# Making the next block's input from the scaled old residual and the scaled y, high parts first

## The chip, the cores and the metric

The kernel runs on one core of one Trainium2 chip. The metric is device time in microseconds (us): the median of several executions. Engines are named as the profile names them: PE (TensorE matmul), PEld (its weight loads), DVE (VectorE), ACT (ScalarE), POOL (GpSimd) and SP (the queue that issues the DMAs).

## What is computed

Two transformer blocks follow each other. The first works on two streams of 256 tokens, `x` and a context; the second on `x` alone. Cut to what matters here, the end of the first block and the start of the second are:

```python
ux = _modulate(_rmsnorm(hx, g[2]), mx[:, 3], mx[:, 4])
yc, yx = _neighbourhood_attention(uc, ux, ...)             # last mixer of the first block
hx = hx + mx[:, 5] * _rmsnorm(yx, g[3])                    # join A
hx = _ffn_sublayer(hx, (mx[:, 6], mx[:, 7], mx[:, 8]), g[4], g[5], ...)   # x alone
# second block, for l in range(2):                           join B stands before l = 0
h = rmsnorm(x, norm_w); proj = h @ w_in
...                                                        # MLA, gated delta rule, MoBA
x = x + y @ w_out                                          # join C: l = 0 into l = 1
```

Everything is fp32. A matmul operand is kept as a high part and a low part, and a product is made of three matmuls: high by high, weight high by input low, weight low by input high.

## The kernel before

The residual `h` lies in SBUF as 8 slices (k = 0 to 7) of 128 features by 256 tokens for `x`. A sublayer leaves its output `y` in two tiles of four slices, and the sums of its squares as matmuls by a matrix of ones into PSUM bank `n`. What joins two sublayers runs in this order where only `x` is left:

- `rstd` (L358): ACT L371 makes a first 1/sqrt from bank `n`, DVE refines it in three steps (L372 to L374). This is r of y.
- `add_normed` (L385): per two slices, DVE multiplies y by the gain column and r (L393, twice 256 wide) and adds it to `h` (L397, 512 wide).
- `scaled` (L444): per slice ACT writes the high part of h times the next norm's gain column (L459) and DVE the low part (L460). The next input's own r is not multiplied in: it is applied behind the matmuls. For it ACT squares two slices of `h` (L64), and `Sums(self, True)` feeds each square to PE at once, two fp32 matmuls by ones per square, eight in all.
- `ffn` (L474) or `hybrid` (L1171) then projects. In `ffn` for `x` alone, f = 0 to 11 first: two weight tiles, two PSUM banks of the tag `ab` (three banks; `ac` has four), 48 matmuls 258 wide, then `part` (L487): DVE multiplies both banks by r (L510, L513), ACT applies Silu, and the result is split again. In `hybrid`, `prn(i)` loads weight i, projects into a `pj` bank (two) or a `gd` bank (three) in 24 matmuls, and DVE multiplies by a copy `rk` of r (L1176, L1182); four-tap convolutions on DVE (L1043), Silu on ACT, the gates and the delta rule follow. The gates' first matmuls are those of L197 into `gd`.

Weights come by DMA as 128x1024 tiles and are split by ACT (high part, L173) and DVE (low part, L174) into a pool of eight tiles, four weights. A scheduler orders the instructions of each engine when the program is built; on the chip every engine takes them strictly in that order.

The three places where this joining happens with `x` alone are called A (neighbourhood attention into the last `ffn`, at about 1620 us), B (that `ffn` into hybrid layer 0, at about 1830 us) and C (hybrid layer 0 into layer 1, at about 2028 us; there is no y norm, only `scaled`).

Of the kernel before, what the change touches and what calls it, by code (L numbers as in the profile page):

```python
# [83 lines left out]
class Net:  # L84
# [359 lines left out]
    def scaled(self, cols, shift=None):  # L444


        nc = self.nc
        u = self.new_u(1 if shift is None else 2)
        if shift is not None:
            for b, s in enumerate(u[1]):  # L450
                self.split(shift[:, 2 * b:2 * b + 2].unsqueeze(2).broadcast_to([128, 2, 2]), s.hi[:, :, 256:258],
                           s.lo[:, :, 256:258])
        ss = Sums(self, True)
        for b in range(4):
            for t in range(2):
                k = 2 * b + t
                hi, lo = self.us(u, k, 0, 256)
                h = self.h[:, k, 0:256]
                nc.scalar.activation(hi, h, AF.Copy, scale=cols[:, k:k + 1])  # L459
                nc.vector.scalar_tensor_tensor(lo, h, cols[:, k:k + 1], hi.bitcast(F), op0=OP.mult, op1=OP.subtract)  # L460
            ss.add(self.hs(0, b, 2))
        return u, ss.rstd()

    def columns(self, r):

# [8 lines left out]
    def ffn(self, n, u, halves, mid, xdone, extra=(), r=None):  # L474
# [9 lines left out]
            s = g[f // 2]  # L484
            return s.hi[:, f % 2, c0:c1], s.lo[:, f % 2, c0:c1]

        def part(f, ws, c0, c1):  # L487
            w = c1 - c0
            if w == 512 or r is not None:
                (pa, pb), ab = [self.bank("ab") for _ in range(2)], None  # L490
            else:
                p = self.bank("ab", (128, 2, 256))
                pa, pb, ab = p[:, 0], p[:, 1], {}
            w2 = w if r is None else w + 2
            for k, p, wt in [(k, *x) for x in zip((pa, pb), ws) for k in range(DT)] if r is None else \
                    [(k, *x) for k in range(DT) for x in zip((pa, pb), ws)]:
                self.mm3([p[:, :w2]], wt.at(lambda x: x[:, k * 128:(k + 1) * 128]), [self.us(u, k, c0, c0 + w2)],
                         k == 0, k == DT - 1, [ab])
            if f // 2 not in g:
                t = self.bp.tile([128, 2080], R, name="b", tag="b")  # L500
# [29 lines left out]
        with self.space("ffn", 6):  # L530
# [10 lines left out]
            def wide(f):  # L541
# [3 lines left out]
                    next(extra)  # L545
                part(f, ws, 0, width)

            for f in range(f0, FA):
                wide(f)

# [40 lines left out]
    def proj(self, src, u, c0, c1, tag="ab", m=128):  # L591
        w = self.weight(src, 8 * m)
        p = self.bank(tag)[:m, :c1 - c0]
        self.project(p, w, u, c0, c1, m)
        return p

    def project(self, p, w, u, c0, c1, m=128, bank=None):
        for k in range(DT):
# [572 lines left out]
    def hybrid(self, l, scaled, prm3):  # L1171
# [4 lines left out]
        nc.vector.tensor_copy(rk, r)  # L1176
        cw, prm, abt = prm3
        W = I["w2"]
        def prn(i, out=None, scale=1.0, tag="pj"):
            p = self.proj(W[l, i], u, 0, 256, tag)  # L1180
            out = self.r1() if out is None else out
            nc.vector.scalar_tensor_tensor(out, p, scale, rk, op0=OP.mult, op1=OP.mult)  # L1182
            return out
# [131 lines left out]
    def program(self):  # L1315
# [14 lines left out]
        with self.psum(pj=2, gd=3, at=2), self.narrow_space(), self.space("hy", 1):  # L1330
            self.second_consts()
            cols = [self.n2[:, l] for l in range(3)]
            if on("s"):
                for l in range(2):
                    self.hybrid(l, self.scaled(cols[l]), prm[l])
                    self.save(f"d_s{l}")
            ss = Sums(self, True)
            for b in range(4):
# [12 lines left out]
    def first_block(self, es, on, ada):  # L1351
# [11 lines left out]
        with self.psum(ab=3, ac=4):  # L1363
# [51 lines left out]
            for i, (name, l, which, factor, halves, run) in enumerate(seq):  # L1415
# [7 lines left out]

                def xdone(y, l=l, which=which, factor=factor, nxt=nxt, box=box):
                    if nxt and nxt[4] == 1 and nxt[0] != "na":
                        link(None, y, 0, (l, which, factor), None)
                        box["u"] = self.scaled(*self.pre_cols(*nxt[1:3], 0))
                    elif nxt:
                        box["u"] = self.new_u()
                        link(box["u"], y, 0, (l, which, factor), nxt[1:3])  # L1430
                    else:
                        link(None, y, 0, (l, which, factor), None)

                yc = run(u, mid, xdone)
                post = (l, which, factor)
# [143 lines left out]
```

## Time and profile before

| | |
|---|---|
| median of 3 runs (lowest, highest) | 2234.25 us (2233.92, 2235.57) |
| the profiled execution: its own time | 2232.82 us |
| the profiled execution: span of the trace | 2230.8 us |
| busy share of the span: PE, PEld | 97%, 84% |
| busy share: DVE, ACT, POOL | 71%, 50%, 0% |
| chain that ended last, by engine | PE 79%, ACT 9%, DVE 9%, issue 1%, DMA 1% |

The trace lists every instruction of one execution with its start, its length and what released its engine if it stood idle before. A window row gives the busy time of each engine in a stretch, and the clock granted to PE as a share of full speed.

### The profile page before, as it was taken

Reading aid. Unit: us, or ns where it says so; the run is one execution under the profiler, and the core shown is the slowest. Engines: PE = TensorE matmul, PEld = TensorE weight load, DVE = VectorE, ACT = ScalarE, POOL = GpSimd, SP = SyncE. Lnnn points to the kernel's source line nnn. Section 1 sums busy time; section 2 is a strip of 40 time slices with the busy share of each in tenths; the row PEclk is TensorE's granted clock in tenths of the full one; section 3 lists DMA queues with packets and bytes.
Section 4 is the critical chain, followed back from the end, with each engine's and each line's share of the span. In section 5 each row is a group of like instructions: output and inputs, shape, how many; then the busy total and the mean of one; then the engine's idle time right before and its main releaser. Section 6 shows DMA issues by size and latency. Waiting matters only on the chain.

```text
span 2230.8 us, 33424 instructions
## 1 busy us (share of the span) xinstructions
PE 2169.8 (97%) x13010; PEld 1878.0 (84%) x13010; DVE 1587.0 (71%) x2899; ACT 1117.2 (50%) x1841; POOL 6.5 (0%) x34
## 2 busy tenths in 40 slices
PE   7999999999999999999999999999999989999997
PEld 4888889877789888889988889977789989888986
DVE  7877674869978876758844454956565668977985
ACT  4422223668867322236622223668754448457744
POOL 0000000000000000000000000000000000000000
PEclk9999999999999999999999999999999999999999
DMA  8556553431135766644554453442346553324331
GB/s 303 194 183 194 181 187 124 155 104 48 38 104 166 227 202 191 196 162 149 189 172 159 161 171 132 152 132 86 109 131 188 170 171 123 114 77 142 120 99 57
DMA packets 96165, 332.76 MB, mean 149 GB/s; under 512 B 12772, under 2 KB 15462, under 8 KB 96008
## 3 DMA queue, kind: packets, MB, share of 16 engines
q1 hardware_dynamic: 96008, 330.64, 45.8%
q8 instruction: 102, 1.67, 0.3%
q14 instruction: 55, 0.45, 0.1%
HBM read 329.55 MB, written 1.05 MB: 148 GB/s over the span
## 4 chain that ended last, share of the span: by engine, by line
PE 79%; ACT 9%; DVE 9%; issue 1%; DMA 1%; SPq 0%; DVEq 0%; ACTq 0%
PE ab L182 36%; PE ac L182 16%; PE ac L186 8%; PE ab L197 5%; PE pj L182 4%; PE gd L182 3%; PE n L182 2%; PE ab L186 2%; ACT w L173 2%; DVE w L174 2%; PE at L182 1%; ACT c L795 1%; DVE y L393 1%; PE gd L186 1%; PE pj L186 1%
## 5 line engine op out<-in xcount | busy, mean ns | idle before, releaser
L173 ACT ACTIVATE w<-raw 128x1024 fp32r<-128x1024 f32 x466 | 489.5, 1053 | 785.1 <-PE ab L182 269.1
L182 PE MATMUL ab<-u,w 128*128 128x512 f32 (+2 forms) x4320 | 870.9, 361 | 4.1 <-ACT u L459 4.1
L182 PEld LDWEIGHTS ab<-u,w 128*128 128x128 f32 x4320 | 729.0, 189 | 126.1 <-ACT u L459 4.5
L174 DVE TENSOR_TENSOR w<-raw,w 128x1024 fp32r<-128x1024 f32 x466 | 565.6, 1216 | 316.2 <-ACT w L173 309.2
L182 PE MATMUL ac<-b,w 128*128 128x512 f32 (+1 forms) x1152 | 233.6, 364 | 0.0
L182 PEld LDWEIGHTS ac<-b,w 128*128 128x128 f32 x1152 | 196.4, 188 | 36.6
L186 PE MATMUL ac<-b,w 128*128 128x256 f32 x1680 | 202.1, 281 | 0.0
L186 PEld LDWEIGHTS ac<-b,w 128*128 128x128 f32 x1680 | 199.9, 189 | 0.8
L182 PE MATMUL pj<-u,w 128*128 128x256 f32 (+1 forms) x1200 | 156.1, 285 | 5.9 <-ACT u L459 4.4
L311 DVE SCALAR_TENSOR_TENSOR ra<-ra,cb 128x1024 f32<-128x1024 f32 x130 | 158.3, 1222 | 4.7 <-ACT cb L1373 2.2
L197 PE MATMUL ab<-u,w 128*128 128x256 f32 x1152 | 147.8, 290 | 7.3 <-ACT u L173 5.8
L182 PEld LDWEIGHTS pj<-u,w 128*128 128x128 f32 (+1 forms) x1200 | 145.5, 187 | 10.8 <-ACT u L459 5.0
L197 PEld LDWEIGHTS ab<-u,w 128*128 128x128 f32 x1152 | 144.0, 197 | 9.2 <-ACT u L173 6.0
L311 DVE SCALAR_TENSOR_TENSOR c<-ra,cb 128x1024 f32<-128x1024 f32 x98 | 118.8, 1219 | 14.2 <-ACT cb L1373 7.0
L507 DVE TENSOR_TENSOR s<-s,ab 128x512 f32<-128x512 f32 (+1 forms) x78 | 47.0, 603 | 90.9 <-PE ab L182 90.4
L182 PE MATMUL ac<-w,u 128*128 128x512 f32 x384 | 90.4, 393 | 0.0
L182 PEld LDWEIGHTS ac<-w,u 128*128 128x128 f32 x384 | 71.7, 188 | 15.4 <-DVE u L174 0.4
L182 PE MATMUL n<-r,ones 128*128 128x256 f32 (+1 forms) x216 | 73.7, 452 | 7.1 <-ACT r L64 2.7
L173 ACT ACTIVATE b<-s 128x512 fp32r<-128x512 f32 (+1 forms) x100 | 53.3, 533 | 29.6 <-DVE s L507 22.5
L174 DVE TENSOR_TENSOR b<-s,b 128x512 fp32r<-128x512 f32 (+1 forms) x100 | 56.2, 562 | 3.1 <-ACT b L173 2.9
L182 PEld LDWEIGHTS n<-r,ones 128*128 128x128 f32 x216 | 36.7, 197 | 19.9 <-DVE r L62 8.2
L64 ACT ACTIVATE r<-h 128x512 f32<-128x512 f32 x56 | 34.9, 626 | 31.4 <-DVE h L397 10.4
(291 smaller groups left out, 2297.0 us busy)
## 6 DMA issues: line engine op xcount, KB each, us to landing
raw<-in_fin SPq DMA_DIRECT2D x194, 512.0 KB, 3.4
raw<-in_fout SPq DMA_DIRECT2D x112, 512.0 KB, 3.4
ra<-in_ada SPq DMA_DIRECT2D x72, 512.0 KB, 4.2
ra<-in_ada0r SPq DMA_DIRECT2D x58, 512.0 KB, 3.5
raw<-in_w SPq DMA_DIRECT2D x54, 512.0 KB, 3.4
raw<-in_da_qk SPq DMA_DIRECT2D x16, 512.0 KB, 3.3
raw<-in_na_qk SPq DMA_DIRECT2D x16, 512.0 KB, 3.4
raw<-in_w2o SPq DMA_DIRECT2D x16, 512.0 KB, 3.4
```

The costliest lines, as they stand in the source:

```text
L64: net.nc.scalar.activation(s, x, AF.Square)
L173: self.nc.scalar.activation(hi, x, AF.Copy)
L174: self.anchor = self.nc.vector.tensor_tensor(lo, x, hi.bitcast(F), op=OP.subtract).ins.name
L182: return mm(out, lhsT, rhs, start=start, stop=stop)
L186: ins = mm(out, lhsT, rhs, start=start and "first" not in bank, stop=stop and bank["done"] == n)
L197: ins = mm(out, lhsT, rhs, start=start, stop=stop)
L311: ins = nc.vector.scalar_tensor_tensor(junk, w, 1.0, self.cb[:, j], op0=OP.mult, op1=OP.mult, accum_out=self.mod[l][:, m, t, j:j + 1])
L393: ins = nc.vector.scalar_tensor_tensor(yy[:, t], yy[:, t], cols[:, k:k + 1], r, op0=OP.mult, op1=OP.mult)
L507: nc.vector.tensor_tensor(s, s, pb, op=OP.mult)
L795: nc.scalar.activation(e[:, j, :nk], s, AF.Exp, bias=mx[:, j:j + 1], accum_out=sm[:, j:j + 1])
```

## The change

At A and B, `join` replaces `add_normed` followed by `scaled`. ACT scales the old residual by the next gain column (`old`, L487) and y by the product of both gain columns (`new`, L489). Once r of y is there, DVE multiplies `new` by it (L493) and adds it to `old` (L494), 512 wide; ACT copies the sum into the high part (L495), and DVE makes all low parts (L498) behind the last high part. Only then do `add_normed` and the norm of the new residual run, and the squares are added up on DVE (L62) ahead of two matmuls by ones in place of eight. `low_last` projects with the high parts of several weights at once and with the low parts after them: f = 0 and f = 1 of the `ffn` together in four banks (two `ab`, two `ac`), and the first three projections of each hybrid layer (two `pj`, one `gd`). C keeps `scaled`, with the squares added on DVE and `low_last`.

```diff
-        ss = Sums(self, True)
+        ss = Sums(self)
+    def join(self, y, ss, post, cols, shift=None):
...
+        both = self.small(DT, "both")
+        nc.vector.tensor_tensor(both, post, cols, op=OP.mult)
...
+        for k in range(DT):
+            nc.scalar.activation(at(old, k), self.h[:, k, 0:256], AF.Copy, scale=cols[:, k:k + 1])
+        for k in range(DT):
+            nc.scalar.activation(at(new, k), at(y, k), AF.Copy, scale=both[:, k:k + 1])
+        r = ss.rstd()
+        for b in range(4):
+            v = two(old, b)
+            nc.vector.tensor_tensor(two(new, b), two(new, b), r.unsqueeze(1).broadcast_to([128, 2, 256]), op=OP.mult)
+            nc.vector.tensor_tensor(v, v, two(new, b), op=OP.add)
+            nc.scalar.activation(self.part_of(u, b)[0], v, AF.Copy)
+        for b in range(4):
+            hi, lo = self.part_of(u, b)
+            nc.vector.tensor_tensor(lo, two(old, b), hi.bitcast(F), op=OP.subtract)
+        self.add_normed(y, r, post, 0)
+        return u, self.norm_r(0)
...
+            if r is not None:
+                ws = [fin(f) for f in range(2)]
+                ps = [[self.bank(tag) for _ in range(2)] for tag in ("ab", "ac")]
+                self.low_last([p[:, :258] for x in ps for p in x], sum(ws, []), u, 0, 258)
+                for f in range(2):
+                    part(f, ws[f], 0, 256, ps[f])
+                f0 = 2
...
+    def low_last(self, ps, ws, u, c0, c1):
+        at = lambda x, k: x[:, k * 128:(k + 1) * 128]
+        for k in range(DT):
+            for p, w in zip(ps, ws):
+                hi = self.us(u, k, c0, c1)[0]
+                self.mm(p, at(w.hi, k), hi, k == 0, False)
+                self.mm(p, at(w.lo, k), hi, False, False)
+        for p, w in zip(ps, ws):
+            for k in range(DT):
+                self.mm(p, at(w.hi, k), self.us(u, k, c0, c1)[1], False, k == DT - 1)
...
+        ws = [self.weight(W[l, i]) for i in range(3)]
+        ps = [self.bank(tag)[:, :256] for tag in ("pj", "pj", "gd")]
+        self.low_last(ps, ws, u, 0, 256)
...
-            p = self.proj(W[l, i], u, 0, 256, tag)
+            p = ps[i] if i < 3 else self.proj(W[l, i], u, 0, 256, tag)
...
-                    self.hybrid(l, self.scaled(cols[l]), prm[l])
+                    self.hybrid(l, self.scaled(cols[l]) if l else self.join(*self.last, cols[0]), prm[l])
...
-                        link(None, y, 0, (l, which, factor), None)
-                        box["u"] = self.scaled(*self.pre_cols(*nxt[1:3], 0))
+                        box["u"] = self.join(*y, self.post_cols(l, which, factor, 0), *self.pre_cols(*nxt[1:3], 0))
```

The scheduler's order moves with it. First ACT at join A, before the change, from the squares of the second half of y to the first high part (`ac` are the banks of that half, `r512` squares, `n` the bank of sums, `r256_14093` r of y, `w` split weights, `u` parts of the next input):

```order
L64 ACTIVATE r512_14080<-ac_13955 128x512
L687 ACTIVATE y_14077<-ac_13955 128x512
L173 ACTIVATE w_14254<-raw_14252 128x1024
L64 ACTIVATE r512_14085<-ac_13956 128x512
L687 ACTIVATE y_14077<-ac_13956 128x512
L371 ACTIVATE r256_14093<-n_13946,eps_78 128x256
L459 ACTIVATE u_14112<-h_81,pa120_14110 128x256 x2
```

The same stretch of ACT with the change:

```order
L64 ACTIVATE r512_14080<-ac_13955 128x512
L749 ACTIVATE y_14077<-ac_13955 128x512
L489 ACTIVATE y_14114<-y_13941,both_14110 128x256 x2
L64 ACTIVATE r512_14085<-ac_13956 128x512
L749 ACTIVATE y_14077<-ac_13956 128x512
L489 ACTIVATE y_14114<-y_13941,both_14110 128x256 x2
L489 ACTIVATE y_14115<-y_14077,both_14110 128x256 x4
L371 ACTIVATE r256_14133<-n_13946,eps_78 128x256
L173 ACTIVATE w_14212<-raw_14210 128x1024
L495 ACTIVATE u_14094<-c4_14112 128x2x256
```

Six scalings of y now stand between the last square and the rstd, and a weight's high part behind the rstd instead of ahead of it; its low part (`w_14213`) stands on DVE between r and the first L493.

Next DVE at join A with the change, from the sum of the third square to the first bank that is read (`ab_14216` holds half of f = 0, `r256_14181` is r of the new residual; `add_normed` and one more low part, `w_14340`, stand ahead of these rows):

```order
L62 TENSOR_TENSOR r512_14166<-r512_14166,r512_14171 128x512
L174 TENSOR_TENSOR w_14346<-raw_14343,w_14345 128x1024
L62 TENSOR_TENSOR r512_14166<-r512_14166 128x256
L62 TENSOR_TENSOR r512_14174<-r512_14174 128x256
L174 TENSOR_TENSOR w_14413<-raw_14410,w_14412 128x1024
L174 TENSOR_TENSOR w_14419<-raw_14416,w_14418 128x1024
L372 SCALAR_TENSOR_TENSOR r512_14174<-n_14178,r256_14181 128x256
L373 SCALAR_TENSOR_TENSOR r512_14174<-r512_14174,r256_14181 128x256
L374 SCALAR_TENSOR_TENSOR r256_14181<-r512_14174,r256_14181 128x256
L174 TENSOR_TENSOR w_14485<-raw_14482,w_14484 128x1024
L552 TENSOR_TENSOR s_14317<-ab_14216,r256_14181 128x256
L553 COPY s_14317<-ab_14216 128x1
```

and PE beside it, where each row of `ab` or `ac` is a number of matmuls and a row of `n` one matmul by ones:

```order
L182 MATMUL ab<-u,w 128x258 x16
L182 MATMUL ac<-u,w 128x258 x16
L182 MATMUL ab<-u,w 128x258 x10
L182 MATMUL n<-r_14166,ones 128x256
L182 MATMUL n<-r_14174,ones 128x256
L182 MATMUL ab<-u,w 128x258 x470
```

Before, the L460s were DVE's last work ahead of the r of the new residual. Now `add_normed`, the sums on DVE and five weights' low parts stand there or just behind, and on PE the sums stand inside f = 2: its first bank takes 24 matmuls into the third `ab` bank (10 ahead of the sums), its second bank is the one that L552 and L553 free.

Last, PE at join B with the change, from the end of `low_last` on (`gd`, `pj` and `at` are projections, L197 `n` turns r into columns):

```order
L182 MATMUL gd<-u,w 128x256 x34
L182 MATMUL at<-u,w 8x256 x2
L182 MATMUL gd<-u,w 128x256 x3
L182 MATMUL n<-r_16594,ones 128x256
L182 MATMUL n<-r_16602,ones 128x256
L182 MATMUL gd<-u,w 128x256 x17
L197 MATMUL n<-ones,r_16609 128x1 x2
L182 MATMUL gd<-u,w 128x256 x2
L182 MATMUL at<-u,w 8x256 x5
L182 MATMUL pj<-u,w 128x256 x48
```

In the kernel before 32 projection matmuls stood ahead of that L197, now 120 do; and the gates' first L197 into `gd` stands 456 projection matmuls into hybrid layer 0 where it stood 491 in.

## Rows read from the trace of the kernel before

**Rows 1.** The page's first part: busy time, share of the span, instructions.

```profile
PE 2169.8 (97%) x13010; PEld 1878.0 (84%) x13010; DVE 1587.0 (71%) x2899; ACT 1117.2 (50%) x1841; POOL 6.5 (0%) x34
```

**Rows 2.** Busy windows: stretch, length, PE, PEld, DVE, ACT, POOL, clock, DMA, GB/s.

```profile
1660.00:1680.00 20.00, 20.00 (x163) 19.60 (x163) 13.32 (x26) 8.87 (x13) 0.00 (x0) 1.00 0.58 180
1850.00:1910.00 60.00, 59.03 (x470) 55.25 (x468) 54.28 (x111) 54.73 (x81) 1.20 (x12) 1.00 0.48 157
1910.00:1950.00 40.00, 37.13 (x280) 34.04 (x279) 37.37 (x102) 15.36 (x26) 0.00 (x0) 1.00 0.32 95
2040.00:2100.00 60.00, 59.92 (x471) 55.80 (x470) 55.36 (x122) 51.67 (x80) 1.00 (x10) 1.00 0.44 141
```

**Rows 3.** Timeline of join A: start, length, engine, line, instruction [idle before, releaser].

```profile
1611.00 10.43 PE L186 MATMUL ac<-o,w 128*128 128x256 f32 x86
...
1622.31 0.58 ACT L64 ACTIVATE r<-ac 128x512 f32<-128x512 f32 x1
...
1622.79 0.59 ACT L687 ACTIVATE y<-ac 128x512 f32<-128x512 f32 x1
...
1624.11 0.47 ACT L371 ACTIVATE r<-n,eps 128x256 f32<-128x256 f32 x1 [0.73 <-PE n L182]
...
1625.99 0.88 DVE L393 SCALAR_TENSOR_TENSOR y<-y,po,r 128x256 f32<-128x256 f32 x2
1626.91 0.69 DVE L397 TENSOR_TENSOR h<-h,y 128x512 f32<-128x512 f32 x1
1627.52 0.87 DVE L393 SCALAR_TENSOR_TENSOR y<-y,po,r 128x256 f32<-128x256 f32 x2
1627.64 0.91 ACT L459 ACTIVATE u<-h,pa 128x256 fp32r<-128x256 f32 x2 [3.05 <-DVE h L397]
...
1628.20 1.23 PE L182 MATMUL ab<-u,w 128*128 128x258 f32 x4 [4.12 <-ACT u L459]
...
1628.45 0.61 ACT L64 ACTIVATE r<-h 128x512 f32<-128x512 f32 x1
...
1634.60 1.02 PE L182 MATMUL n<-r,ones 128*128 128x256 f32 x4
```

**Rows 4.** Busy windows within join A (columns as in rows 2).

```profile
1626.00:1628.00 2.00, 0.00 (x0) 0.00 (x0) 1.97 (x5) 0.36 (x1) 0.00 (x0) 0.50 0.11 45
...
1631.00:1632.00 1.00, 1.00 (x4) 0.82 (x4) 1.00 (x4) 0.79 (x2) 0.00 (x0) 0.50 0.00 0
...
1633.00:1634.00 1.00, 1.00 (x8) 0.90 (x7) 1.00 (x3) 1.00 (x3) 0.00 (x0) 1.00 0.00 0
```

**Rows 5.** The chain that ended last, behind join A: start, length, what.

```profile
1635.62 69.76 PE ab L182 x562
```

**Rows 6.** Timeline of join B and hybrid layer 0.

```profile
1833.11 0.47 ACT L371 ACTIVATE r<-n,eps 128x256 f32<-128x256 f32 x1 [1.56 <-PE n L182]
...
1837.20 0.79 PE L182 MATMUL pj<-u,w 128*128 128x256 f32 x2 [4.13 <-ACT u L459]
...
1847.29 0.41 DVE L1182 SCALAR_TENSOR_TENSOR xp<-pj,rk 128x256 f32<-128x256 f32 x1
...
1850.77 1.28 ACT L1044 ACT_TABLE_LOAD   x1
...
1852.06 0.42 ACT L1044 ACTIVATE c<-r 128x256 f32<-128x256 f32 x1
...
1879.94 1.22 DVE L174 TENSOR_TENSOR w<-raw,w 128x1024 fp32r<-128x1024 f32 x1
1881.07 0.48 DVE L1043 SCALAR_TENSOR_TENSOR r<-xp,cw,r 128x256 f32<-128x256 f32 x1
...
1906.74 2.90 PE L197 MATMUL gd<-c,r 128*128 128x256 f32 x18
```

**Rows 7.** Timeline of join C and hybrid layer 1.

```profile
2030.20 0.50 PE L182 MATMUL pj<-u,w 128*128 128x256 f32 x2 [0.27 <-ACT u L459]
...
2040.09 0.42 DVE L1182 SCALAR_TENSOR_TENSOR xp<-pj,rk 128x256 f32<-128x256 f32 x1
...
2093.19 1.04 PE L197 MATMUL gd<-c,r 128*128 128x256 f32 x6
```

More of the change, by code (lines that the diff above doesn't have):

```diff
@@ L462, in scaled, with part_of @@
         return u, ss.rstd()
+    def part_of(self, u, b):
+        g, ts = u
+        s = ts[2 * b // g]
+        c = slice(2 * b % g, 2 * b % g + 2)
+        return s.hi[:, c, 0:256], s.lo[:, c, 0:256]
+    def join(self, y, ss, post, cols, shift=None):
+        nc = self.nc
+        u = self.new_u(1 if shift is None else 2)
+        if shift is not None:
+            for b, s in enumerate(u[1]):
+                self.split(shift[:, 2 * b:2 * b + 2].unsqueeze(2).broadcast_to([128, 2, 2]), s.hi[:, :, 256:258],
+                           s.lo[:, :, 256:258])
+        both = self.small(DT, "both")
+        nc.vector.tensor_tensor(both, post, cols, op=OP.mult)
+        old = [self.c4() for _ in range(2)]
+        new = [self.yp.tile([128, 4, 256], F, name="y", tag="y") for _ in range(2)]
+        at = lambda x, k: x[k // 4][:, k % 4]
+        two = lambda x, b: x[b // 2][:, 2 * (b % 2):2 * (b % 2) + 2]
+        for k in range(DT):
[13 more added lines that the diff above has]
+        return u, self.norm_r(0)
     def columns(self, r):
@@ L485, in gat, with part @@
             return s.hi[:, f % 2, c0:c1], s.lo[:, f % 2, c0:c1]
-        def part(f, ws, c0, c1):
+        def part(f, ws, c0, c1, ps=None):
             w = c1 - c0
-            if w == 512 or r is not None:
+            if ps:
+                pa, pb = ps
+            elif w == 512 or r is not None:
                 (pa, pb), ab = [self.bank("ab") for _ in range(2)], None
@@ L494, in part @@
             w2 = w if r is None else w + 2
-            for k, p, wt in [(k, *x) for x in zip((pa, pb), ws) for k in range(DT)] if r is None else \
-                    [(k, *x) for k in range(DT) for x in zip((pa, pb), ws)]:
-                self.mm3([p[:, :w2]], wt.at(lambda x: x[:, k * 128:(k + 1) * 128]), [self.us(u, k, c0, c0 + w2)],
+            if not ps:
+                order = [(k, *x) for x in zip((pa, pb), ws) for k in range(DT)] if r is None else \
+                    [(k, *x) for k in range(DT) for x in zip((pa, pb), ws)]
+                for k, p, wt in order:
+                    self.mm3([p[:, :w2]], wt.at(lambda x: x[:, k * 128:(k + 1) * 128]), [self.us(u, k, c0, c0 + w2)],
                          k == 0, k == DT - 1, [ab])
@@ L1431, in xdone @@
                     else:
-                        link(None, y, 0, (l, which, factor), None)
+                        self.last = (*y, self.post_cols(l, which, factor, 0))
                 yc = run(u, mid, xdone)
```

## The prediction

> **What bounds the kernel now.** I read the page's busy shares first: PE is busy for 97% of the span [rows 1]. Then the busy windows. Inside the last `ffn` PE is busy for all 20 of 20 us while DVE is busy for 13.3 and ACT for 8.9: there time is matmuls, and whatever holds PE up counts in full. In the hybrid layers PE has 59.0 of 60 us, but DVE has 54.3 and ACT 54.7, and behind that DVE has 37.4 of 40 us against PE's 37.1 [rows 2]: three engines are almost equally full, and work that is moved onto DVE finds little room. Last the timelines of the three joins. At A the last matmul of y ends at 1621.44; PE then does sums and stands idle for 4.12 us until 1628.20, waiting for ACT's first high part, which waited for DVE's new residual [rows 3]. That gap, and eight fp32 sums of squares between the first projections (four records last 1.02, which are two matmuls, so 0.51 each), are what the change goes for. The reader is to see the price of one step: two 256-wide scalings on ACT take 1628.45 - 1627.64 = 0.81, a 512-wide DVE operation holds DVE for 1627.52 - 1626.91 = 0.61, a pair of L393 for 0.92 [rows 3], a low part of a weight for 1881.07 - 1879.94 = 1.13 [rows 6], a matmul 258 wide in a stream for 69.76 / 562 = 0.124 [rows 5].
>
> **Join A, the start.** ACT now scales y between the squares and the rstd. The last square starts at about 1622.0, a little earlier than 1622.31, since two scalings stand ahead of it in place of a weight's high part; the copy of y follows 0.5 later, and six scalings from 1623.0 take 2.43. L371 starts at about 1625.4 instead of 1624.11. From L371 to the first DVE product it was 1625.99 - 1624.11 = 1.88, so 1627.3; but the low part of the fourth weight now stands there, 1.13, so 1628.4. Two products and the first sum (0.61 + 0.61 + 0.69) and a 512-wide copy on ACT (0.61) follow: PE starts at **1630.95, 2.75 later than before** [rows 3, 6]. The step that was to start PE sooner starts it later.
>
> **Join A, the stream.** PE then has 96 matmuls without a sum in between, 11.9 us. The clock costs on top: while PE stood idle the granted clock fell to 0.50, the lower of its levels (1.2 of 2.4 GHz), was there still in 1631 to 1632, over 3 us after the restart, and was 1.00 in 1633 to 1634 [rows 4]. Before, the waits for the new residual covered that; now nothing does, and I take 2.0 us: half of the four slow ones. The 96 end at 1644.9, and 24 more go into the third `ab` bank.
>
> **Join A, the r that comes late.** The second bank of f = 2 is the one that f = 0 holds until DVE multiplies it by r of the new residual. DVE's order up to there, from 1628.4: eight products and sums at 0.61 (1633.3), four low parts of the input at 0.61 (1635.7), `add_normed` 4 x (0.92 + 0.61) = 6.1 (1641.8), the sums of squares, two at 0.61 and two half as wide, about 2.0 (1643.8), four low parts of weights 4.5 (1648.3), three refinements of 0.46 (1649.7). Waits add some 1.4: the pool holds four weights, all four are in `low_last`, and the fifth can be split only when the first is done with (72 matmuls, 1641.9, and ACT's high part of about 1.1). A fifth low part of 1.13 and the reading of the bank, 0.57, bring it to 1652.8; the last 24 matmuls of f = 2 end at 1655.8. Before, 14 of these 144 matmuls were done at 1635.62 and 130 x 0.124 = 16.1 more ended at 1651.7 [rows 5]. **A costs 4.1 us.** Without the waits and the fifth low part it is 1.5; with another 2 us of waiting for weights, 6. Behind it f = 3 finds its banks read, and nothing in this `ffn` can take the time back [rows 2].
>
> **Join B.** Eight scalings, 3.24, stand ahead of the rstd; 1.56 of them lie in ACT's wait for the sums [rows 6], so L371 is 1.7 late (1834.8), and with 1.88 + 1.22 + 0.69 + 0.61 PE starts at 1839.2 instead of 1837.20. The 72 matmuls of `low_last` and 48 more cover PE up to r, about as far as PE came before in the same time. DVE is another matter. From 1836.7: 4.9, 2.4, 6.1 and 2.0 as at A (1852.1), three low parts of weights 3.4 (1855.5), waits for their high parts about 0.8, and the last sum on PE, L371, the refinement and the copies of r about 3.6: the first product by `rk` starts at 1859.9 instead of 1847.29, **12.6 late**. Those low parts and a small one were done after 1847.29 before, so 3.6 of it is only moved. Left is 9.0, against DVE's idle time: 60 - 54.28 = 5.7 up to 1910 and 40 - 37.37 = 2.6 up to 1950 [rows 2]. If all of it can be filled, B costs 0.6; if none, 9.0. Much of it is waiting for an ACT and a PE that are as full, but the order has been drawn up afresh for the late start: I take 3.5, nearer the lower end.
>
> **Join C.** No y norm here: PE starts as before at 2030.20 [rows 7] and saves six fp32 sums, 6 x 0.51 = 3.1. DVE gets the sums (2.0) and two low parts (2.3) ahead of r, less some 0.7 that r waited for PE's sums: the first product by `rk` comes 3.6 later than 2040.09, of which 2.3 is moved. Left is 1.3. Counted in the two orders, hybrid layer 1 has four more table loads on ACT (23 for 19), two of them ahead of the gates. In the trace a load lasts 1.28, and the next activation starts 1852.06 - 1850.77 = 1.29 after its start [rows 6]: 2.6 more on an ACT that has 8.3 idle of 60 [rows 2]. Between -3.1 (PE's saving is kept) and +3.9 (1.3 + 2.6) I take +1.0, since DVE has only 4.6 us idle there. Layer 0 has one more load, which lies in B's range.
>
> The Trainium skill's page "ScalarE: Activation LUTs", section "What ACT_TABLE_LOAD costs", speaks harder against the change: a load of about 1283 ns, and with a drain of about 1380 ns some 2.66 us for each switch. By that C's two loads would hold ACT for 5.3 in place of 2.6, and the time below would be 2245.6. The trace agrees with the 1283 and has no room for a drain between load and activation; I leave that case a chance of 0.02.
>
> **The sum** against the profiled execution's own 2232.82: 4.1 + 3.5 + 1.0 = 8.6, so 2241.4. The median of the runs is 1.43 above that execution, so 2242.9, and I say 2243.
>
> **The rivals.** *DVE's idle time cannot be filled* in the hybrid layers, since each idle piece waits for a convolution's ACT step: B 9.0, C 3.9, with A 17.0, 2251. For it: ACT has 54.7 of 60 [rows 2]. Against it: the scheduler's new order. Chance 0.12. *The hybrid layers absorb it*: DVE fills every gap, B 0.6, and PE keeps its 3.1 at C: with A +1.6, 2236. For it: PE is busy for 59.9 of 60 us in layer 1 [rows 2], so that PE may be the bound there. Chance 0.22. *Faster, through the gates*: the order has moved them ahead of the last convolutions. In layer 0 DVE has seven taps (0.48), two products by `rk` (0.41) and seven low parts (1.13) less to do before them, 12.1 us; with its 5.7 idle filled they would start at 1906.74 + 12.6 - 12.1 - 5.7 = 1901.5, 5.2 earlier; in layer 1, by the same count (two, one and three, 4.8), at 2093.19 + 3.6 - 4.8 - 4.6 = 2087.4, 5.8 earlier [rows 6, 7]. If the chain behind the gates alone sets the layer's end, that is 4.1 - 11.0 = -6.9, 2227. It decides only if that chain has no more than its own work: from 1910 on DVE is busy for 37.4 of 40 us [rows 2], and the convolutions put behind the gates come on top. Chance 0.12. That the change would not do what it says is excluded by the order: the high parts do run first.
>
> **How the numbers follow.** A difference under 0.2% (4.5 us) is what a measurement of this kernel cannot tell from none. My forecast has 0.52; with the rival that fills nothing (0.12) and the drain (0.02), slower has 0.66; no difference 0.22; faster 0.12. The range from 2232 to 2250 leaves out the faster rival and half of the slowest one; at its lower end lies the case in which A costs 1.5 and the hybrid layers give 3.
>
> **What would show it.** In the changed profile: at A, L371 a good microsecond later against the end of y's matmuls, PE's first matmul 9 to 10 us behind that end (6.8 before), and a PE wait of 2 to 4 us named L553, in the middle of f = 2. At B, the first product by `rk` more than 20 us behind PE's first projection instead of 10. No such wait at A, and PE's first matmul within 6.5 us, would make the prediction wrong at its main term; the gates' matmuls 5 us nearer to the join, with the layer's end drawn along, would make it wrong in sign.

## The result and the profile after

The changed kernel takes 2254.73 us (median of 4 runs, 2254.13 to 2255.14) against 2234.09 for the kernel before in the same session (2233.65 to 2235.57). The ratio is 1.0094, with a 95% interval from 1.0082 to 1.0106: slower by 20.6 us where 8.6 were forecast, and above the range of 2232 to 2250. The sign was right, the size was not.

The page's first part hardly moves against [rows 1]: PE is busy for 0.1 us less, DVE for 13.5 more, ACT for 16.7 more.

```profile
PE 2169.7 (96%) x12974; PEld 1878.8 (83%) x12974; DVE 1600.5 (71%) x2921; ACT 1133.9 (50%) x1870; POOL 6.5 (0%) x34
```

So PE is busy for as long as before, although 18 fp32 sums are gone from it (36 matmul records fewer, some 9 us at 0.51 each), and stands idle for 21.6 us more. The busy windows say where (columns as in rows 2; the stretches of the hybrid layers are moved by 14 us, by which the first product by `rk` in layer 0 and the start of layer 1 come later): the ffn is as full as it was [rows 2], both hybrid layers have lost about 4 of 60 us of PE, and DVE and ACT are hardly fuller than before.

```profile
1660.00:1680.00 20.00, 20.00 (x163) 19.47 (x162) 13.52 (x29) 10.27 (x15) 0.00 (x0) 1.00 0.52 164
1864.00:1924.00 60.00, 54.78 (x396) 49.86 (x395) 53.10 (x117) 54.96 (x81) 1.24 (x12) 0.94 0.39 123
1924.00:1964.00 40.00, 36.04 (x267) 32.84 (x266) 36.43 (x98) 13.45 (x21) 0.00 (x0) 0.96 0.31 93
2054.00:2114.00 60.00, 56.33 (x446) 52.16 (x446) 54.87 (x118) 52.99 (x76) 1.01 (x10) 1.00 0.46 150
```

**Three stages.** I cut the span at four marks: the end of y's last matmul at A, the end of y's last matmul of the ffn, PE's first projection of hybrid layer 1, and the end. Timeline of the kernel before, where the rows ahead do not have it: y's last matmuls in the ffn, and in each layer the last convolution on DVE and the start of the inversion (`gd` by `ident`):

```profile
1818.05 11.39 PE L186 MATMUL ac<-b,w 128*128 128x256 f32 x94
...
1904.80 0.48 DVE L1043 SCALAR_TENSOR_TENSOR r<-xp,cw,r 128x256 f32<-128x256 f32 x1
...
1942.35 1.06 PE L218 MATMUL gd<-ident,gd 128*128 128x128 f32 x8 [0.67 <-DVE gd L1113]
...
2093.27 0.48 DVE L1043 SCALAR_TENSOR_TENSOR r<-xp,cw,r 128x256 f32<-128x256 f32 x1
...
2129.63 1.03 PE L218 MATMUL gd<-ident,gd 128*128 128x128 f32 x8
```

and of the changed kernel:

```profile
1610.17 10.51 PE L186 MATMUL ac<-o,w 128*128 128x256 f32 x86
...
1820.92 11.35 PE L186 MATMUL ac<-b,w 128*128 128x256 f32 x94
...
1841.95 1.22 PE L182 MATMUL pj<-u,w 128*128 128x256 f32 x4 [6.04 <-ACT u L495]
...
1861.33 0.74 DVE L1249 SCALAR_TENSOR_TENSOR xp<-pj,rk 128x256 f32<-128x256 f32 x2
...
1915.95 0.47 DVE L1105 SCALAR_TENSOR_TENSOR r<-xp,cw,r 128x256 f32<-128x256 f32 x1
...
1955.41 1.90 PE L218 MATMUL gd<-ident,gd 128*128 128x128 f32 x8 [3.26 <-DVE gd L1175]
...
2044.08 0.74 PE L182 MATMUL pj<-u,w 128*128 128x256 f32 x4 [0.25 <-ACT u L459]
...
2057.50 0.74 DVE L1249 SCALAR_TENSOR_TENSOR xp<-pj,rk 128x256 f32<-128x256 f32 x2
...
2110.51 0.48 DVE L1105 SCALAR_TENSOR_TENSOR r<-xp,cw,r 128x256 f32<-128x256 f32 x1
...
2150.57 1.94 PE L218 MATMUL gd<-ident,gd 128*128 128x128 f32 x8 [3.26 <-DVE gd L1175]
```

Start plus length of the last matmul is the mark: A lasted 1829.44 - 1621.43 = 208.01 and now 1832.27 - 1620.68 = 211.59; B 2030.20 - 1829.44 = 200.76 and now 211.81; C 200.60 and now 208.22. **A costs 3.6, B 11.1, C 7.6**; with 0.75 gained ahead of A, where nothing was changed, that is the 21.5 between the spans.

The same rows divide B and C. In B, PE starts 1.9 later behind y's last matmul (9.68 for 7.76). The last convolution ends 74.47 us behind that start where it ended 68.08 behind it: 6.4. From there to the inversion it is 38.99 for 37.07: 1.9. The rest is 0.8. In C: 66.91 for 63.55, 3.4; 39.58 for 35.88, 3.7; the rest 0.6.

What PE did in B and C is read from the busy windows of the two whole stages, of the kernel before

```profile
1829.44:2030.20 200.76, 187.98 (x1369) 166.75 (x1368) 164.60 (x397) 123.71 (x210) 1.20 (x12) 0.99 0.35 111
2030.20:2230.80 200.60, 187.92 (x1376) 166.84 (x1376) 161.53 (x391) 116.42 (x202) 1.00 (x10) 0.99 0.30 98
```

and of the changed kernel, with two stretches out of them:

```profile
1832.27:2044.08 211.81, 190.70 (x1357) 169.05 (x1356) 170.92 (x406) 126.76 (x215) 1.24 (x12) 0.96 0.33 106
2044.08:2252.33 208.25, 188.24 (x1364) 166.81 (x1364) 163.36 (x395) 121.46 (x206) 1.01 (x10) 0.97 0.29 94
...
1888.00:1893.00 5.00, 4.82 (x22) 4.82 (x23) 3.98 (x6) 4.97 (x8) 0.00 (x0) 0.50 0.33 105
...
2151.00:2156.00 5.00, 5.00 (x20) 3.77 (x19) 4.39 (x10) 1.97 (x4) 0.00 (x0) 0.50 0.00 0
```

PE stands idle 8.3 us longer in B (length less busy time: 21.1 for 12.8) and 7.3 longer in C (20.0 for 12.7). It is also busy 2.7 and 0.3 longer, although six fp32 sums are gone from each, because the granted clock is 0.50 for a while behind PE's waits: at the restart of B up to 1846, behind waits for two weights near 1888, and behind a wait of 3.26 ahead of the inversion in both layers. Half of PE's busy time in these stretches, less the one that B had before, is my estimate of what the clock costs: 5.1 us in B and 3.1 in C. By this account the sums that are gone give 2.4 and 2.8 back.

At A the steps that were forecast can be seen one by one (timeline):

```profile
1622.12 2.51 ACT L489 ACTIVATE y<-y,both 128x256 f32<-128x256 f32 x6
...
1624.52 0.48 ACT L371 ACTIVATE r<-n,eps 128x256 f32<-128x256 f32 x1
...
1626.29 1.22 DVE L174 TENSOR_TENSOR w<-raw,w 128x1024 fp32r<-128x1024 f32 x1
1627.42 1.29 DVE L493 TENSOR_TENSOR y<-y,r 128x512 f32<-128x512 f32 x2
...
1630.03 1.23 PE L182 MATMUL ab<-u,w 128*128 128x258 f32 x4 [7.07 <-ACT u L495]
...
1650.08 0.15 DVE L553 COPY s<-ab 128x1 f32<-128x1 f32 x1
...
1650.37 14.90 PE L182 MATMUL ab<-u,w 128*128 128x258 f32 x108 [2.78 <-DVE s L553]
```

PE starts 9.35 us behind y's last matmul (6.77 before, [rows 3]), and stands for 2.78 in f = 2, for the bank that L553 frees. The windows show what each of the two waits costs on top (the column behind POOL is the clock):

```profile
1632.00:1634.00 2.00, 2.00 (x11) 2.00 (x11) 2.00 (x4) 0.99 (x2) 0.00 (x0) 0.50 0.00 0
1634.00:1635.00 1.00, 1.00 (x8) 1.00 (x7) 1.00 (x3) 0.00 (x0) 0.00 (x0) 0.69 0.00 0
1635.00:1636.00 1.00, 1.00 (x11) 1.00 (x10) 0.96 (x3) 0.00 (x0) 0.00 (x0) 1.00 0.00 0
...
1652.00:1653.00 1.00, 1.00 (x7) 1.00 (x6) 0.60 (x2) 1.00 (x3) 0.00 (x0) 0.50 0.78 320
...
1655.00:1656.00 1.00, 1.00 (x10) 1.00 (x9) 1.00 (x4) 0.75 (x1) 0.00 (x0) 0.95 0.00 0
```

The granted clock is 0.50 from the restart to past 1634, as forecast, and falls to 0.50 once more behind the wait in f = 2, where nothing of the kind was forecast: 14.90 us for 108 matmuls that take 13.4 at 0.124.

### The profile page after: what moved, and what is told of

Its sections match the earlier page's. It is cut to its first block, busy times and chain, and to the rows that moved or that the text cites. A ratio compares the mean times of both kernels' runs of the same rounds, so it can differ in the third digit from the quotient of the medians.

```text
span 2252.3 us, 33402 instructions
## 1 busy us (share of the span) xinstructions
PE 2169.7 (96%) x12974; PEld 1878.8 (83%) x12974; DVE 1600.5 (71%) x2921; ACT 1133.9 (50%) x1870; POOL 6.5 (0%) x34
## 4 chain that ended last, share of the span: by engine, by line
PE 78%; ACT 10%; DVE 9%; DMA 1%; issue 1%; SPq 0%; DVEq 0%; ACTq 0%
PE ab L182 35%; PE ac L182 16%; PE ac L186 7%; PE ab L197 5%; PE pj L182 5%; PE gd L182 3%; PE ab L186 2%; DVE w L174 2%; ACT w L173 2%; PE n L182 2%; PE at L182 1%; ACT c L857 1%; PE gd L186 1%; DVE y L393 1%; PE pj L186 1%
## 5 line engine op out<-in xcount | busy, mean ns | idle before, releaser
L173 ACT ACTIVATE w<-raw 128x1024 fp32r<-128x1024 f32 x466 | 489.3, 1053 | 778.4 <-PE ab L182 266.2
L174 DVE TENSOR_TENSOR w<-raw,w 128x1024 fp32r<-128x1024 f32 x466 | 565.6, 1217 | 322.7 <-ACT w L173 317.0
L182 PE MATMUL pj<-u,w 128*128 128x256 f32 (+1 forms) x1200 | 160.9, 289 | 14.9 <-ACT u L495 6.0
L197 PE MATMUL ab<-u,w 128*128 128x256 f32 x1152 | 147.0, 289 | 8.0 <-ACT u L173 6.8
L197 PEld LDWEIGHTS ab<-u,w 128*128 128x128 f32 x1152 | 143.5, 196 | 9.7 <-ACT u L173 7.1
L182 PE MATMUL n<-r,ones 128*128 128x256 f32 (+1 forms) x180 | 61.9, 447 | 7.2 <-ACT r L379 2.3
L173 ACT ACTIVATE b<-s 128x512 fp32r<-128x512 f32 (+1 forms) x100 | 53.2, 533 | 28.0 <-DVE s L549 20.8
L174 DVE TENSOR_TENSOR b<-s,b 128x512 fp32r<-128x512 f32 (+1 forms) x100 | 56.1, 562 | 3.1 <-ACT b L173 2.9
L372 DVE SCALAR_TENSOR_TENSOR r<-n,r 128x256 f32<-128x256 f32 (+1 forms) x48 | 25.5, 531 | 32.1 <-ACT r L371 32.0
```

The source lines that it names most:

```text
L173: self.nc.scalar.activation(hi, x, AF.Copy)
L174: self.anchor = self.nc.vector.tensor_tensor(lo, x, hi.bitcast(F), op=OP.subtract).ins.name
L182: return mm(out, lhsT, rhs, start=start, stop=stop)
L197: ins = mm(out, lhsT, rhs, start=start, stop=stop)
L372: nc.vector.scalar_tensor_tensor(v, p, EPS * n, r, op0=OP.add, op1=OP.mult)
```

## The experiments

Joins A, B and C lie one behind the other, so one run can try a different piece in each; each is read by its own stage. The table gives the stages of one profiled execution each, as differences to the profiled kernel before, and the median of the runs. A stage that was left as before came out between -0.2 and +1.6 in other runs: what is under 1.5 in one stage says little. A single stretch at clock 0.50 far behind a join is enough for that: in C of e8 one from 2182.3 to 2185.7, far behind layer 1's inversion, costs 1.7, half of the time that PE was busy in it.

| run | A | B | C | median |
|---|---|---|---|---|
| the change | +3.6 | +11.1 | +7.6 | 2254.7 |
| e1: joins, no low_last at A and B; C direct sums, low_last | +10.0 | +11.6 | +1.0 | 2255.9 |
| e2: low_last at A and B, no joins; C sums on DVE, no low_last | -0.6 | -2.1 | +9.2 | 2239.1 |
| e3: A with four `ac` banks; rest as before | -0.7 | +0.9 | +1.6 | 2234.2 |
| e4: A as e3, r of y first; B join, r of y first; C as before | -3.7 | +11.2 | +1.2 | 2241.1 |
| e5: the change, Exps behind the last Silu | +2.4 | +8.4 | +4.5 | 2248.5 |
| e6: before, last Silu behind the first Exp | -0.2 | +4.2 | +5.1 | 2240.6 |
| e7: A as e4; B join with r earlier, low_last; C low_last, direct sums | -3.5 | +4.1 | 0.0 | 2233.7 |
| e8: A as e4; B without join; low_last and direct sums in both layers | -3.9 | -2.3 | +1.2 | 2227.8 |
| e9, e10: e8, r late by 3 and 1, by 6 and 3 copies | -3.4, -3.6 | -0.8, -0.1 | +0.1, -0.2 | 2229.0, 2229.5 |
| e11: e8, 3.7 us of DVE work ahead of r | -3.3 | -2.2 | +6.0 | 2233.4 |
| e12: e8, r late by 16 and 8 copies | -3.6 | +6.7 | +2.1 | 2238.2 |
| e13: e8, 3.7 us of DVE work behind r | -3.6 | +4.4 | +5.9 | 2238.8 |
| e14: e8 with C's sums on DVE | -3.5 | -0.9 | +3.8 | 2232.1 |

The kernel before had medians of 2232.3 to 2233.5 in these sessions. e7 and e9 to e14 carry the rule of order of e5; e8 does not.

### Which part costs: e1 and e2

```diff
# e1: ffn and layer 0 weight by weight, direct sums at C
-            if r is not None:
+            if False:                 # ffn, f = 0 and 1
+        if l == 1:                    # hybrid: low_last in layer 1 alone
# e2: the other halves
-    box["u"] = self.join(...)
+    link(None, y, 0, (l, which, factor), None)
+    box["u"] = self.scaled(..., direct=True)
```

> Joins A and B keep the new order of the join, but the ffn and hybrid layer 0 project weight by weight as before (no high parts of several weights first). Join C gets its squares straight to PE as before, and layer 1 keeps the high parts first. Read at three marks: the sums of y in front of B (1831.08 in the kernel before, 1833.92 with the change), PE's first projection of layer 1 (2030.20, 2044.08) and the end of the span (2230.8, 2252.3). Theory one, the late r is what costs: A is dearer than in the change, since f = 1 now needs a bank that f = 0 holds until r: about +10 at the first mark; B still costs about 10 up to the second mark, since r is as late; C costs 0 to 1, since its r is not late. Rival, the three weights projected together are what costs: B costs 2 (the later start of PE alone), C 7.

> The other half: A and B add to the residual and scale as before, with direct sums, and the ffn and hybrid layer 0 take the high parts of several weights first; at C the squares are added on DVE, and layer 1 projects weight by weight as before. Theory one (late r): A -0.5 to +0.5, since r is there before a bank is wanted; B 0 to 1; C +3 to +7, because its r is late. Rival (weights projected together): A 0, B about +9, C 0 to 1. Third: both are dear, and each gives some 5.

B and C fall cleanly apart. B costs 11.6 with the join alone and gives 2.1 with `low_last` alone; C costs 1.0 with `low_last` and direct sums and 9.2 with the sums on DVE alone. The high parts first are harmless in both layers; **the join, which adds its squares on DVE, costs B, and the sums on DVE cost C**. In B of e1 and e4 and in C of e2 the order has also put a Silu between two Exps, whose price is taken apart below. At A the join without `low_last` costs 10.0, as expected, and PE's longest wait behind its start names the bank that is late (timeline of e1):

```profile
1651.57 13.69 PE L182 MATMUL ab<-u,w 128*128 128x258 f32 x90 [2.92 <-DVE s L553]
```

### Join A: e3 and e4

```diff
-                ps = [[self.bank(tag) for _ in range(2)] for tag in ("ab", "ac")]
+                ps = [[self.bank(tag) for _ in range(2)] for tag in ("ac", "ac")]
# e4, in join:
+        r = ss.rstd()
         for k in range(DT):
             nc.scalar.activation(at(new, k), at(y, k), AF.Copy, scale=both[:, k:k + 1])
-        r = ss.rstd()
```

> A as in the change, but f = 0 and f = 1 both take their two banks from the tag ac, so that f = 2 finds all three ab banks free; B, C and the hybrid layers as in the kernel before. My theory of A: the wait for r in f = 2 goes away, PE starts as late as in the change; A costs 3.8 - 2.8 = 1.0 in place of 3.8, and the time is about 1 us above the kernel before. Rival: the wait comes back at f = 3 or at a weight, then A costs 3 or more.

> A as in the last one and the join of B (without the high parts first in layer 0), C as before; in both joins r of y is asked for ahead of the scalings of y, so that L371 stands on ACT ahead of four (A, B) of them, and no low part of a weight stands on DVE between r and the product. If the scalings and that low part are what makes PE start late at A: its first projection comes about 2.5 earlier, some 7 us behind the end of y's matmuls instead of 9.4, and A costs 1.0 - 2.5 = -1.5. B: PE starts 1.6 earlier than in the change, 0.3 after the time of the kernel before; by theory one the layer still loses about 8, since r of the new residual is no earlier by more than that; by the rival it loses 0 to 1.

With four `ac` banks the wait in f = 2 is gone and A costs -0.7, 4.3 less than in the change: the 2.78 of the wait and the 1.5 of half clock behind it. With r of y first, PE starts 2.5 earlier and A gains 3.7 (timeline of e4; y's last matmul ended at 1620.20):

```profile
1622.53 0.47 ACT L371 ACTIVATE r<-n,eps 128x256 f32<-128x256 f32 x1
...
1624.41 1.29 DVE L493 TENSOR_TENSOR y<-y,r 128x512 f32<-128x512 f32 x2
...
1627.03 9.26 PE L182 MATMUL ac<-u,w 128*128 128x258 f32 x62 [4.53 <-ACT u L495]
```

The step of the change that was to start PE sooner still does not (6.83 behind y's last matmul, 6.77 before). What A gains lies behind the start: six of the eight fp32 sums are gone, 3.1 us by their count and 0.51 each. By the windows of stage A PE stands idle as long as before (4.87 for 4.81) and is busy 3.8 less; in e2, which keeps the eight sums, it is 0.6 less. B in e4 loses 11.2 although PE starts there only 0.4 later: its start is not what is dear.

### The place of one Silu: e5 and e6

The rows above name PE's wait of 3.26 ahead of the inversion in both layers. ACT shows why it is there: in the change, layer 1, the Silu of the last convolution (L1106) stands between two Exps of the gates (L1133, L1134), and each time a table is loaded.

```profile
2110.48 1.28 ACT L1133 ACT_TABLE_LOAD   x1
2111.77 0.39 ACT L1133 ACTIVATE gd<-gd 128x256 f32<-128x256 f32 x1
2112.18 1.28 ACT L1106 ACT_TABLE_LOAD   x1
2113.47 0.42 ACT L1106 ACTIVATE c<-r 128x256 f32<-128x256 f32 x1
2113.91 1.28 ACT L1134 ACT_TABLE_LOAD   x1
2115.20 0.28 ACT L1134 ACTIVATE gd<-gd 128x128 f32<-128x128 f32 x1
```

e5 orders the eight Exps behind that Silu; e6 does the reverse to the kernel before.

```diff
# e5, in delta_rule
-            nc.scalar.activation(qkv[i // 4][:, i % 4], y, AF.Silu)
+            silu = nc.scalar.activation(qkv[i // 4][:, i % 4], y, AF.Silu).ins.name
-            nc.scalar.activation(dec0[:, h], b[:, 0:256], AF.Exp)
-            nc.scalar.activation(dec1[:, h], b[:, 256:384], AF.Exp)
+            for e in (nc.scalar.activation(dec0[:, h], b[:, 0:256], AF.Exp),
+                      nc.scalar.activation(dec1[:, h], b[:, 256:384], AF.Exp)):
+                self.after(e, silu)
# e6: the last Silu after the first Exp (h = 0) instead
```

> The changed kernel with one rule for the order on ACT: in both hybrid layers the gates' eight Exps stand behind the Silu of the last convolution (in the change the first Exp stands ahead of it, so that Exp, Silu, Exp need two table loads more). Four table loads fewer in all. Read from the last convolution on DVE to the first matmul of the inversion (gd by ident): 37.6 and 36.3 us in layers 0 and 1 before, 39.5 and 40.1 with the change. If the place of that Silu is a cause of its own, both stretches fall by at least 2 x 1.28 = 2.6 and the time by 5, to 2249 or 2250. Rival, the late r explains everything and the loads lie beside other work: the time stays within 1.5 of 2254.7.

> The kernel before with the opposite rule: in both hybrid layers the Silu of the last convolution stands behind the first Exp of the gates, all else as before (r as early as before). If the place of the Silu is a cause of its own: 2.6 to 3.8 more per layer, 2239 to 2241. Rival: nothing, 2233 to 2235.

Both ways it is a cause of its own. PE's wait of 3.26 is 1.09 and 1.17 in e5. In e5 the stretch from the last convolution to the inversion falls to 34.0 in both layers, B costs 2.7 less and C 3.1 less, and the ratio to before is 1.0070 (1.0055 to 1.0085). In e6, B is 4.2 and C 5.1 slower with nothing else changed, ratio 1.0030 (1.0018 to 1.0041). Its two loads are 2.6 of that in each layer. The rest is not clear of noise: the interval is 4 to 9 us for both layers together, the profiled execution was the slowest of seven (2243.7, median 2240.6), and in layer 0 the stretch up to the inversion grew by 2.2 alone (5.1 in layer 1). PE stands idle 2.1 and 3.3 longer in the two stages, about the loads; another 1.7 in each is the clock, at 0.50 behind the waits (1949 to 1951, 2119 to 2122). The same place in e5:

```profile
2109.91 0.42 ACT L1106 ACTIVATE c<-r 128x256 f32<-128x256 f32 x1 [0.56 <-DVE r L1105]
2110.35 1.28 ACT L1133 ACT_TABLE_LOAD   x1
2111.64 0.39 ACT L1133 ACTIVATE gd<-gd 128x256 f32<-128x256 f32 x1
```

The Trainium skill's page "ScalarE: Activation LUTs", section "Table sets: the hidden batching unit", says to do the activations of one table set together. These two runs agree: in their profiles one Silu out of place is worth 2.7 to 5.1 us a layer.

### What is left of B: e7 and e8, then r made late by itself

e7 keeps the join at B, but makes r of the new residual earlier; e8 leaves the join out there and has no rule of order.

```diff
# e7, join at B: residual and norm ahead of the low parts, squares straight to PE
-        for b in range(4):
-            ... low parts (L498)
         self.add_normed(y, r, post, 0)
-        return u, self.norm_r(0)
+        n = self.norm_r(0, direct=True)
+        for b in range(4):
+            ... low parts
+        return u, n
# e8, against e7
-  self.join(*self.last, cols[0])                # layer 0
+  self.scaled(cols[0], direct=True)
```

> Joins A and B as in the run with r of y first and four ac banks, and low_last in ffn and both layers; at B, add_normed and the norm of the new residual stand ahead of the low parts of the input, and its squares go straight to PE; Exps behind the Silu as in the run above; C with direct squares. A -3.7 as measured. At B the first product by rk should stand some 15 us behind PE's first projection (10.1 before, 19.4 with the change). If the lateness of r is what is left of B's cost: between 3 and 6 in place of 11.0. If what costs is that the join is there at all (its extra passes on DVE and ACT): 8 or more. C 0 to 1.5.

> The parts that gained so far: A by the join with r of y first and f = 0, 1 in four ac banks (-3.7); at B and C the old way with direct squares, and low_last in both hybrid layers (B -2.1, C about 0). Theory: 2233 - 3.7 - 2.1 = 2227 to 2228, about 0.25% faster than the kernel before. Rival: the pieces measured are no larger than the spread of a layer that nothing was changed in (0.9 to 1.6 us), then 2230 to 2233.

e7: the first product by `rk` stands 16.5 us behind PE's first projection in place of 19.4, and B costs 4.1 in place of 11.1 (8.4 with the Silu in its place); 1.5 of that is PE's earlier start, since r of y is asked for first. e8 is faster than both kernels: **ratio 0.9977 to before, 0.9968 to 0.9987**. Then, on e8, r made late with no work for DVE, ACT or PE:

```diff
# e9, e10, e12, in hybrid; n copies in layers 0 and 1: (3, 1), (6, 3), (16, 8)
         u, r = scaled
+        for _ in range(n[l]):
+            late = self.r1()
+            nc.gpsimd.tensor_copy(late, r)
+            r = late
# e11: six sums on DVE that nobody reads, beside the squares ahead of r; e13: behind the second Silu
+                nc.vector.tensor_tensor(junk, ..., op=OP.add)
```

> The last run's kernel (join at A only, low_last in both layers, direct squares), Exps behind the last Silu, and nothing else but a later r: POOL, which is idle, copies r of the new residual to another tile three times ahead of layer 0 and once ahead of layer 1. Nothing is added to DVE, ACT or PE. The first product by rk stood 13.9 and 11.9 us behind PE's first projection without the copies. If a late r is what costs, each layer loses about as much as its r comes later beyond the last run (layer 0 against -2.3, layer 1 against +1.2). Rival, what costs is the work that the join and the sums add to DVE and ACT: nothing is lost.

> The same with six copies ahead of layer 0 and three ahead of layer 1: a second point of the line. Late r: the loss grows one for one with the delay of the first product by rk. Rival: no loss.

> The rival by itself: no copies, but in front of each hybrid layer six sums on DVE (512 wide, 0.61 each, 3.7 in all) whose results nobody reads, at the place of the squares. If DVE's load costs, each layer loses about 3.7 against the run without them; if only the lateness of r costs, as much as the first product by rk comes later, which may be less, since r waits for PE's sums meanwhile.

> The copies on POOL last 0.44 us each, and the delay of the two runs before was swallowed: the first product by rk came no more than 0.6 later than without them. So sixteen copies ahead of layer 0 (7.1 us) and eight ahead of layer 1 (3.5), nothing else changed; no work is added to DVE, ACT or PE. If a late r costs by itself: the first product by rk comes 4 to 6 us later in layer 0 (at some 18 to 20 us behind PE's first projection) and 2 to 3 later in layer 1, and each layer loses at least as much. Rival, only work on DVE and ACT costs: -1 to +2 against the run without copies in each layer.

e9 and e10 decide nothing: the delay was 0.4 to 2.7 us, and the product by `rk` came at most 0.6 later. In e8 DVE waits 2.54 in layer 0 and 1.48 in layer 1 between the copies of r and that product, for a weight's high part (L173); the delay went into these waits. e12 decides for layer 0. Its copies, PE's wait for the columns of r, and DVE's product (timeline), and a window behind that wait:

```profile
1842.46 9.09 POOL L1239 COPY r<-r 128x256 f32<-128x256 f32 x16 [28.57 <-DVE r L374]
...
1851.60 1.01 PE L197 MATMUL n<-ones,r 1*128 1x1 f32 x4 [4.20 <-POOL r L1239]
...
1852.99 0.74 DVE L1254 SCALAR_TENSOR_TENSOR xp<-pj,rk 128x256 f32<-128x256 f32 x2
```

```profile
1852.00:1857.00 5.00, 5.00 (x24) 4.99 (x25) 4.54 (x11) 3.00 (x5) 0.20 (x2) 0.50 0.31 108
```

The product stands 19.9 us behind PE's first projection, as late as with the join, and B costs 6.7. e9 and e10 are the same kernel but for the number of copies, with the product at 14.4 and 14.0: against them e12 costs 7.6 and 6.9 more for 5.5 and 5.9 of lateness. Some 2.7 of that is the clock, at 0.50 from PE's restart at 1851.6 up to 1857. (Against e8 it is 9.1 for 6.0, but e8 has not the rule of order, nor the stretch at 0.50 near 2000 that e9, e10 and e12 have, far behind the join.) In e5, with the join, the product stands at 20.1, and B costs 8.4, of which 1.9 is PE's later start: 6.5. **At B the price of the join is, within the spread of a stage, the late r.** e11 says the same from the other side: 3.7 us of sums on DVE that nobody reads, ahead of r, do not make the product later in layer 0 (13.7), and cost nothing there. In order of that product, B is -2.2 at 13.7 (e11), -2.3 at 13.9 (e8), -0.1 at 14.0 (e10), -0.8 at 14.4 (e9), -0.9 at 14.9 (e14), +4.1 at 16.5 (e7), +6.7 at 19.9 (e12). Up to about 14 a later product costs nothing: with `low_last` it comes 3.8 later than before (10.1), and yet the last convolution of e8 ends 2.6 earlier behind PE's first projection (65.5 for 68.1).

### What is left of C: e11 to e14

> As the run with six idle sums on DVE in front of each layer, but the six sums (3.7 us) stand behind the second convolution, in the chain of the convolutions, where they can't make r late. If DVE is the bound of this stretch: 3 to 4 more in each layer than in the best kernel. If DVE has gaps there that take them: 0 to 1.

> The best kernel with one change back: the squares at C are added on DVE (and Exps stand behind the last Silu). By the run with Exps behind the Silu, where C cost 4.5: +3 to +4.5 against the best kernel, with the first product by rk 1.5 later. If the pieces of C in that run came from elsewhere: 0 to 1.

In layer 1 the stages say less. r late by 3.1 through POOL costs 0.9 (e12 against e8), but C of e8 holds the 1.7 of lower clock far behind the join that e12 does not have: by the windows PE stands idle 2.6 longer in e12, and the inversion starts 104.1 behind PE's first projection where it was 99.3. 3.7 us of DVE work ahead of r, which make it 2.6 late, cost 4.8 against e8 (e11), with the inversion at 104.5. The same work behind r, with r on time, costs 4.7 in layer 1 and 6.7 in layer 0 (e13). That is not the work alone: in both layers the order has put another Silu (L1266, of a gate) between the first two Exps, with two loads, and from the last convolution to the inversion e13 takes 3.5 and 3.7 longer than e8. Up to the last convolution, 3.7 us of DVE work in the chain cost 5.4 in layer 0 and 4.4 in layer 1. The sums on DVE by themselves are 2.6 dearer than direct ones in the stage of C (e14 against e8), 3.6 against e9, which has the same rule of order, and 4.5 in e5. That the sums cost C is shown; how their price splits between DVE's time and r is not.

## Why the prediction was wrong

**Join A, the start: right.** L371 came 1.2 us later behind y's last matmul, PE's first matmul 9.35 behind it (forecast 9.5), and e4 shows that it was the scalings and the low part ahead of the product.

**Join A, the stream and the late r: right in kind; in the sum partly by luck.** The wait of 2 to 4 us at L553 was 2.78; half clock lasted from the restart at 1630.0 into the stretch from 1634 to 1635, as it was taken to. The prediction took this for a cost that only the change has; it was not: before, PE was busy without a wait from 1629 to 1632 at 0.50 as well (the last of these microseconds is in [rows 4]), with the sums of squares. Counted from y's last matmul, the bank came free 1.7 earlier than forecast (1650.37 where 1652.8 was forecast for a y that ends 0.75 later), and the last 24 matmuls of f = 2 took 4.45, to 1654.8, where 3.0 were forecast, since half clock behind the second wait, 1.5, had not been thought of. The two nearly cancel: 4.1 forecast, 3.6 measured.

**Join B: the step that failed is the sum's 3.5, "nearer the lower end".** PE's start was right (2.0 forecast, 1.9), and the first product by `rk` stood 11.2 later behind y's last matmul (29.06 for 17.85) where 12.6 were forecast. But the 9.0 that were left were set against DVE's idle time of 5.7 and 2.6 as if it could be filled. It was not: DVE is idle for more of the new windows than in [rows 2] (6.9 of 60, 3.6 of 40). The idle pieces are a chain's waits, and lateness at the head of the chain goes through to the end. The last convolution ended 6.4 + 1.9 = 8.3 later, close to the 9.0 of the rival that fills nothing. On PE this shows as waits: apart from the start, 1.12, 0.62, 1.79 and 2.04 us of layer 0 go to weights whose parts DVE (L174) or ACT (L173) makes late; before, there was one such wait up to the last convolution, of 0.91.

**Joins B and C: two terms were missing.** The clock behind PE's waits was priced at A and put at nothing in the hybrid layers, without a reason; by the windows it cost 5.1 us at B and 3.1 at C. And the sum priced the table loads ahead of the gates at C, by number, and not which instruction stands between them. The earlier gates were even a rival for the faster side. They did not come early, but 4.3 later behind y's last matmul in layer 0 and 1.3 later behind PE's first projection in layer 1: the last Silu was put among their Exps, and that cost 2.7 and 3.1 us (e5).

**Join C: 1.0 forecast, 7.6 measured; the step that failed is "3.6 later ..., of which 2.3 is moved. Left is 1.3".** r came 3.5 later behind PE's start, as forecast, and the last convolution ended 3.4 later: nothing of what was moved came back. Most of the rest is the Silu, 3.1. PE's saving in sums was kept, 2.8 by the windows, and eaten by 7.3 more of standing idle and 3.1 of lower clock; 3.6 of the idle time is waiting for weights (timeline of the change):

```profile
2094.07 2.83 PE L182 MATMUL pj<-u,w 128*128 128x256 f32 x22 [0.95 <-DVE w L174]
...
2098.50 0.50 PE L182 MATMUL pj<-u,w 128*128 128x256 f32 x2 [1.60 <-ACT w L173]
...
2100.07 8.44 PE L182 MATMUL pj<-u,w 128*128 128x256 f32 x70 [1.07 <-DVE w L174]
```

Split by e5 into what is left without the misplaced Silu and the Silu, the measured sum is A 3.6, B 8.4 + 2.7, C 4.5 + 3.1: 22.3; with the 0.75 gained ahead of A that is the 21.5 of the spans (20.6 in the medians).

## What to carry to other kernels

Where a chain through three engines sets the end, idle time in a window is no reserve: price a late start at its head at one for one or more, until a run shows less (with `low_last` alone 3.8 cost nothing), and add the lower clock behind each new wait of PE. When an edit shifts a scheduler's order, look at which activations now stand between two of another table near that chain; one rule of order was worth 6 us here (e5), and it did not keep another Silu out in e13. And ask for the scalar that everything waits for (r) ahead of the work that merely prepares its use: that swap, with banks that do not need the later r, made the same join 3.7 us better than the old one at A.

## What was not expected of the hardware

A wait of 2.78 us on PE cost another 1.5: the clock was still 1.00 in the first microsecond after it and 0.50 from about 1652 to 1655. In the hybrid layers waits of 1.79 and 3.26 were followed by 0.50 too (1888 to 1893, 2151 to 2156). A table load takes 1.28; one activation in the wrong place, with two loads, cost 4.2 and 5.1 us of a layer in the profile of e6, of which 1.7 each is such a stretch at 0.50. A copy of 128x256 fp32 on POOL takes 0.44 to 0.45 where three or six stand in a row, and 0.57 where sixteen do (9.09 in all).
